# A two-layer diffusion transformer block on one core: the state-space mixer in three parts

## Chip, cores and metric

The kernel runs on one core of one Trainium2 chip. The metric is the device time of one execution in microseconds (us); lower is better. The kernel before has a median of 3212.48 us over 3 runs (3210.45 to 3216.32). TensorE is written PE (its weight loads PEld), VectorE DVE, ScalarE ACT, GpSimdE POOL, SyncE SP.

## What is computed

Two layers over 1024 tokens and 256 context tokens, 1024 channels. Layer 0 mixes by attention and retention, layer 1 by a state-space model (S5). Each layer ends with a squared-ReLU network. The change is in layer 1 and in what stands just before and after it:

```python
h_l = modulate(rmsnorm(x, norm1_g[l]), mod_l[:, 0], mod_l[:, 1])
h_c = modulate(rmsnorm(xc, norm1_g[l]), mod_c[0], mod_c[1])
...
def s5_mixer(h_c, h_l, p_f, p_b, d_skip, w_glu, need_ctx):
    ...
    y_cf, x_cf = s5_scan(u_c, ab_f, bb_f, c_f, x0)
    y_cb, x_cb = s5_scan(u_c[:, ::-1], ab_b, bb_b, c_b, x0)
    y_lf, _ = s5_scan(u_l, ab_f, bb_f, c_f, x_cf)
    y_lb, _ = s5_scan(u_l[:, ::-1], ab_b, bb_b, c_b, x_cb)
    out_l = s5_out(y_lf + y_lb[:, ::-1], u_l, d_skip, w_glu, h_l.dtype)
...
z = jax.nn.gelu(y).astype(dtype) @ w_glu
za, zb = jnp.split(z, 2, axis=-1)
return za * jax.nn.sigmoid(zb)
```

There are 64 groups of 16 channels with 64 complex states each. A state goes through the context and then through the tokens, once forward and once backward; the backward direction also begins with the context (reversed) and then takes the tokens from the last to the first. Context outputs of layer 1 are not needed.

## The kernel before

**Layout.** The residual x lies in SBUF as channels on partitions, 8 tiles (kt, oc) of 1280 columns: tokens 0 to 511 (block 0), tokens 512 to 1023 (block 1), context (block 2). Every large product is done in three passes of split operands (`mm3`, lines 70 to 72: high x high, low x high, high x low). Weights come by `split` (one transfer of 512 KB on SP at L1004, then the high part on ACT at L76 and the low part on DVE at L84), with three raw buffers.

**Networks.** `mlp` goes over 16 pairs of hidden tiles. `first` makes two hidden tiles (ReLU on ACT at L1053, squares, low part on POOL), `second` adds their share to the 8 output tiles; the sum goes from PSUM into x on DVE at L1070, unless the output is in `kept` and stays in its PSUM bank to the end. The network of layer 0 runs in two passes: blocks 0 and 2 (with six outputs of block 2 kept), then block 1 (three outputs kept).

**Side work.** While a network runs, a generator is stepped by `beat`: RA (0.07) steps per matrix product of 512 columns in the first pass, RB (0.125) in the second. The side work is, in order: modulation vectors of layer 1 (`ada_rest`, DVE), the S5 tables (`s5_gen`: powers, input and output matrices, lag matrices, cosines and sines, all written to DRAM tensors bst, cst, tst, csd), and the normalized inputs of blocks 0 and 2 (`s5_in`). What is left of it is drained after the second pass.

**The mixer's form.** Eight tokens make a chunk (128 token chunks, 32 context chunks). Within a chunk a 128x128 lag matrix Tt per group gives the direct part. Between chunks, states are turned by cosines and sines so that the recurrence becomes a real scan over chunks with decay R8. `s5_in` writes the inputs to the DRAM tensor ud, context twice, so that one row of 192 columns serves both directions (context, tokens, context).

**`s5_main`.** It runs alone on the core, 32 steps q of two groups. Per step: SP loads input matrices B, tables CS, output matrices C and two lag matrices Tt three steps ahead; ACT spreads CS (L1493, L1494); `states` does for each direction d four products of 160 columns (128x64 tiles, L1503), then on DVE a product with the tables (L1511), a sum (L1512) and two scans of 160 (L1516), and on DVE or POOL the turning back of 128 chunks (L1519); `outs`, two steps later, adds two lag products (L1531) and 32 products of 64x64 tiles (L1537: state half k times time half h, so all four quarters of the array). After four steps ACT takes two PSUM banks through GELU (L1542) into the tiles Y[kt, th]; th says which four of the eight places in a chunk.

**After it.** `glu` runs over th = 0, 1: 4 transposes per tile (L1573), split into yT (L76, L84), then 16 weight tiles of the gated product; sigmoid, gate, sum into x (L1592). Because of the order by place in the chunk, x is read with a stride of eight there and in the network of layer 1 (`xh`). Modulation rows 3, 4 and 5 of layer 1 are made beside `glu`.

**Order.** Instructions go to each engine in program order, and side work is put between the products where `beat` or `next(side)` stands. SP's queue is in order as well: a load that waits for a buffer holds back what is behind it.

## Time and profile before

| | |
|---|---|
| median of 3 runs | 3212.48 us |
| profiled execution, its own time | 3215.43 us |
| span of the profiled execution | 3213.6 us |
| mean granted clock of PE | 0.967 |
| DMA, mean of the span | 101 GB/s |

The page gives busy time of each engine over the span, and 40 slices of it. The timeline shows where the stages lie: layer 0's mixing up to about 1054 us, its network from there to 2080 us (second pass from about 1700), the normalization of block 1 to 2102, `s5_main` to 2285, `glu` to about 2500, the network of layer 1 to the end. In a row of groups the columns are line, engine, operation, output and inputs with their shapes, count, then busy time and mean of one in ns, then the engine's idle time before them and what ended it. In a row of waits: who waited, for whom, total, times, longest. A row of stages gives the busy time of each engine in the stretch, the granted clock, the DMA share and GB/s.

### The profile page before, as it was taken

What the parts mean: (1) busy time and instruction counts of PE and PEld (TensorE: products, weight loads), DVE (VectorE), ACT (ScalarE), POOL (GpSimd) and SP (SyncE); (2) the same over time, 40 slices, a digit from 0 to 9 for tenths busy, and PEclk for the clock granted to TensorE, in tenths of its full rate; (3) what the DMA queues carried; (4) which work ended last, traced back from release to release, by engine and by line L of the source; (5) the groups of instructions that cost most, each with busy time, mean ns of one, the idle gap of its engine ahead of it and who ended that gap; (6) DMA issues with size and microseconds to landing.
All of it is one profiled execution on the core that took longest, in us unless ns stands there. A gap on an engine that the chain in (4) does not pass through costs nothing. (4 is left out here: it accounts for less than half of the span.)

```text
span 3213.6 us, 45368 instructions
## 1 busy us (share of the span) xinstructions
PE 2968.0 (92%) x16683; PEld 2436.2 (76%) x16683; DVE 2111.0 (66%) x4014; ACT 1221.5 (38%) x2493; POOL 929.7 (29%) x902
## 2 busy tenths in 40 slices
PE   5899998899999998999997999967799999999998
PEld 3777777678878787887785778756678788888887
DVE  6777777687754688556468974378865555555555
ACT  6542222666762332222233664321334322222221
POOL 3642222455540113466326110123222111111111
PEclk8999999999999999999998999979999999999999
DMA  7132222301021452245426555287742111111111
GB/s 250 69 119 84 76 79 63 84 26 25 13 85 34 136 162 89 87 120 154 131 85 206 172 163 145 85 180 196 231 139 89 56 46 53 53 46 47 46 46 66
DMA packets 259039, 324.28 MB, mean 101 GB/s; under 512 B 72336, under 2 KB 179632, under 8 KB 258816
## 3 DMA queue, kind: packets, MB, share of 16 engines
q1 hardware_dynamic: 198352, 281.03, 29.0%
q10 hardware_dynamic: 59264, 36.84, 3.7%
q0 software_dynamic: 1200, 3.51, 0.4%
q8 instruction: 131, 2.15, 0.3%
q14 instruction: 92, 0.75, 0.1%
HBM read 267.96 MB, written 53.35 MB: 100 GB/s over the span
## 5 line engine op out<-in xcount | busy, mean ns | idle before, releaser
L84 POOL TENSOR_TENSOR al<-r,ah 128x512 fp32r<-128x512 f32 (+1 forms) x160 | 204.3, 1289 | 1191.5 <-ACT r L1057 1116.7
L1070 DVE SCALAR_TENSOR_TENSOR x<-b,mods,x 128x512 f32<-128x512 f32 (+1 forms) x483 | 457.5, 967 | 101.1 <-PE b L72 95.1
L84 DVE TENSOR_TENSOR ul<-mraw,uh 128x512 fp32r<-128x512 f32 x256 | 204.6, 803 | 429.3 <-ACT uh L76 428.7
L70 PE MATMUL b<-ah,dh 128*128 128x512 f32 (+1 forms) x1088 | 416.1, 383 | 21.4 <-ACT r L1053 10.2
L71 PE MATMUL b<-al,dh 128*128 128x512 f32 (+1 forms) x1088 | 413.7, 380 | 0.7 <-POOL al L84 0.7
L72 PE MATMUL b<-ah,dl 128*128 128x512 f32 (+1 forms) x1088 | 412.7, 380 | 0.5 <-DVE dl L84 0.4
L76 ACT ACTIVATE uh<-mraw 128x512 fp32r<-128x512 f32 x256 | 160.3, 628 | 453.3 <-PE b L71 261.3
L70 PE MATMUL b<-h2h,uh 128*128 128x512 f32 (+1 forms) x768 | 280.7, 366 | 21.8 <-DVE x L1070 11.6
L72 PE MATMUL b<-h2h,ul 128*128 128x512 f32 (+1 forms) x768 | 278.9, 364 | 18.6 <-DVE ul L84 18.4
L71 PE MATMUL b<-h2l,uh 128*128 128x512 f32 (+1 forms) x768 | 277.5, 361 | 0.0
L70 PEld LDWEIGHTS b<-ah,dh 128*128 128x128 f32 x1088 | 206.7, 190 | 64.8 <-DVE x L1070 11.6
L72 PEld LDWEIGHTS b<-ah,dl 128*128 128x128 f32 x1088 | 206.5, 190 | 40.5 <-DVE dl L84 1.9
L71 PEld LDWEIGHTS b<-al,dh 128*128 128x128 f32 x1088 | 207.0, 190 | 38.1 <-POOL al L84 1.1
L76 ACT ACTIVATE dh<-mraw 128x512 fp32r<-128x512 f32 x192 | 117.5, 627 | 248.2 <-PE b L71 119.6
L84 POOL TENSOR_TENSOR pl<-pe,ph 128x512 fp32r<-128x512 f32 (+1 forms) x128 | 158.3, 1246 | 154.9 <-ACT ph L76 86.8
L70 PE MATMUL b<-h3h,uh 128*128 128x512 f32 x512 | 202.0, 395 | 0.0
L71 PE MATMUL b<-h3l,uh 128*128 128x512 f32 x512 | 200.0, 391 | 2.0 <-DVE h3l L313 1.8
L72 PE MATMUL b<-h3h,ul 128*128 128x512 f32 x512 | 200.9, 393 | 0.0
L70 PEld LDWEIGHTS b<-h2h,uh 128*128 128x128 f32 x768 | 146.6, 191 | 50.5 <-DVE x L1070 14.2
L84 DVE TENSOR_TENSOR dl<-mraw,dh 128x512 fp32r<-128x512 f32 x192 | 150.5, 794 | 48.5 <-ACT dh L76 28.9
L72 PEld LDWEIGHTS b<-h2h,ul 128*128 128x128 f32 x768 | 146.4, 191 | 47.1 <-DVE ul L84 23.7
L1053 ACT ACTIVATE r<-b 128x512 f32<-128x512 f32 (+1 forms) x160 | 87.9, 550 | 244.9 <-PE b L72 170.8
(421 smaller groups left out, 7171.3 us busy)
## 6 DMA issues: line engine op xcount, KB each, us to landing
mraw<-in_w SPq DMA_DIRECT2D x192, 512.0 KB
aw<-in_adat SPq DMA_DIRECT2D x112, 256.0 KB
mraw<-in_glu SPq DMA_DIRECT2D x32, 512.0 KB
aw<-in_adat SPq DMA_DIRECT2D x96, 128.0 KB
CS<-csd SPq DMA_DIRECT2D x32, 320.0 KB
w<-in_adaw SPq DMA_DIRECT2D x32, 256.0 KB
wraw<-in_winr SPq DMA_DIRECT2D x32, 256.0 KB
cst<-oc ACTq DMA_DIRECT2D x64, 128.0 KB
```

The lines of the kernel that those rows point to most:

```text
L70: mm(o, s[0], m[0], start=start, stop=False)
L71: mm(o, s[0], m[1], start=False, stop=False)
L72: mm(o, s[1], m[0], start=False, stop=stop)
L76: self.nc.scalar.activation(o, x, AF.Copy)
L84: e.tensor_tensor(o, x, h.bitcast(F32), ALU.subtract)
L1053: nc.scalar.activation(r[:, :n], b[:, :n], AF.Relu)
L1070: nc.vector.scalar_tensor_tensor(o, as_x(b), self.M[:, l, 5, oc, s:s + 1], xs, op0=ALU.mult, op1=ALU.add)
```

## The change

The mixer is cut into three parts.

- `s5_first`, at the end of the side work beside the network's second pass: for each q the context in both directions (their end states go to the SBUF tensor `carry`) and the first 64 token chunks forward. Its sums go into Y[0, kt] without GELU. It starts when blocks 0 and 2 are normalized; a gate (`half`) keeps `s5_in` back until the network's first pass is written out.
- `s5_second`, alone: the last 64 chunks in both directions, from the carries; forward and backward share one PSUM bank, one scan of 260 columns, with a decay table that is zero at each start.
- `s5_third`, stepped by `next(side)` in `glu`'s first half: the first 64 chunks backward, added to Y[0, kt], and GELU at the end.

`s5_sums` multiplies state half k into output half k alone (64 chunks fit 64 rows). Y tiles now hold 512 consecutive tokens, so `glu` takes th = 1 first and x is read contiguously (`xh` is gone); the weights' rows are permuted on the host to match, and the transposes become 16 products of 64x64 tiles per tile, written with a stride. ud has 160 columns and another order, and `s5_in` writes each tile by eight transfers. RA becomes 0.09, RB 0.14; no output of block 1 is kept in PSUM; modulation rows 3 and 4 of layer 1 move to the side work of the first network. The loads of `s5_second` stand behind the last normalization and the rest of the side work.

```diff
-RA = 0.07
-RB = 0.125
+RA = 0.09
+RB = 0.14
...
 def s5_in(self, bi, x, tmp, b=None):
-            rows = self.ud[kt * P:(kt + 1) * P]
-            for c0 in ((32 + t0 // 8,) if t0 < NL else (0, 160)):
-                nc.sync.dma_start(rows[:, :, c0:c0 + nchunk], us.rearrange("p (s c) -> p s c", s=8))
+            for s in range(8):
+                nc.sync.dma_start(bass.AP(tensor=self.ud.tensor,
+                                          offset=self.ud.offset + 163840 * s + 1280 * kt + c0,
+                                          ap=[[160, 8], [10240, 16], [1, m]]), us[:, m * s:m * s + m])
...
+    def s5_spread(self, CS):
+        self.nc.scalar.activation(CS[:, 0], CS[:, 3], AF.Copy, scale=-1.0)
+        self.nc.scalar.activation(CS[:, 1], CS[:, 2], AF.Copy)
+
+    def s5_decay(self, o, mask, q, d):
+        self.nc.scalar.activation(o, mask, AF.Copy, scale=self.R8[:, 2 * q + d:2 * q + d + 1])
+
+    def s5_sums(self, o, q, k, y, C, start, stop):
+        mm = self.nc.tensor.matmul
+        R = slice(64 * k, 64 * k + 64)
+        for r, w in ((0, 0), (1, 0), (0, 1), (1, 1)):
+            mm(o[R, (q % 4) * P:(q % 4 + 1) * P], y[R, r, w], C[R, w], start=start and r + w == 0,
+               stop=stop and r + w == 2)
+
+    def s5_first(self):
...
+        def states(q):
...
+            for r in range(2):
+                for k in range(2):
+                    R = slice(64 * k, 64 * k + 64)
+                    mm(vb[R, P * r:P * r + 96], B[:, 0, r, R], u[:, k], start=True, stop=True)
+                    mm(vb[R, P * r + 96:P * r + P], B[:, 1, r, R], u[:, k, 31::-1], start=True, stop=True)
...
+        def outs(q):
...
+            for k in range(2):
+                mm(o[64 * k:64 * k + 64, (q % 4) * P:(q % 4 + 1) * P], u[:, k, 32:96], Tt[:, k], start=True, stop=False)
+                self.s5_sums(o, q, k, y, C, False, True)
...
+        for q in range(35):
+            if q < 32:
+                load(q)
+            yield
+            if 1 <= q < 33:
+                states(q - 1)
+            yield
+            yield
+            if q > 2:
+                outs(q - 3)
+            yield
...
+    def s5_second(self, p, last, rest):
...
+            CS = p.tile([P, 4, 2, 65], F32, tag="CS", name="CS", bufs=6)
...
+            v.tensor_tensor_scan(fl(z), fl(dec), fl(S), 0.0, ALU.mult, ALU.add)
...
+            for d in range(2):
+                for k in range(2):
+                    self.s5_sums(o, q, k, A[q, d], C[:, d], False, d == 1)
...
+        ut = p.tile([P, 64, 64], F32, name="ut")
         for _ in range(3):
             next(last)
-        inputs(0, 8)
         self.drain(last)
+        self.drain(rest)
+        for q in range(5):
+            load(q)
+            if q % 4 == 0:
+                inputs(2 * q, 8)
...
+    def s5_third(self, p):
...
+            CS = p.tile([P, 4, 65], F32, tag="CS", name="CS", bufs=3)
...
+            for k in range(2):
+                self.s5_sums(bank[0], q, k, A[q], C, True, True)
...
+        for q in range(35):
+            if q < 32:
+                load(q)
+            yield
+            if 1 <= q < 33:
+                states(q - 1)
+            yield
+            if q > 2:
+                outs(q - 3)
+            yield
+        for kt in range(KT):
+            nc.scalar.activation(self.Y[0, kt], self.Y[0, kt], self.gelu)
...
 def glu(self, p, x, after, sides):
-        for th in range(2):
+        for th in (1, 0):
...
-                for t in range(4):
-                    nc.tensor.transpose(tp[:, t * P:(t + 1) * P], self.Y[kt, th][:, t * P:(t + 1) * P], self.ident)
+                for t in range(8):
+                    for k in range(2):
+                        R, C = slice(64 * k, 64 * k + 64), slice(64 * t, 64 * t + 64)
+                        nc.tensor.matmul(tp[R, C], Y[R, C], self.ident[R, R], start=True, stop=True)
...
-                        if kt % 4 == 3:
-                            next(side, None)
+                        next(side, None)
...
+            self.drain(side)
...
 def run(self, stop=None):
-            yield from self.ada_rest(lambda: self.atile(name="aw"), rows, [(1, j) for j in range(3)])
+            yield from self.ada_rest(lambda: self.atile(name="aw"), rows, [(1, j) for j in range(5)])
             self.s5_setup(gp)
             yield from self.s5_gen(gp)
+            while not half:
+                yield
             for bi in (0, 2):
                 yield from self.s5_in(bi, x, tmp)
+            yield from self.s5_first()
...
-            self.mlp(0, mp, [(512, 512, 0)], hget2, x0, beat, after=st1.add,
-                     kept=[(512, oc) for oc in range(3)])
-        self.drain(side)
...
+            self.mlp(0, mp, [(512, 512, 0)], hget2, x0, beat, after=st1.add)
...
-            self.s5_main(p, self.s5_in(1, x, AT, st1.b))
+            self.s5_second(p, self.s5_in(1, x, AT, st1.b), side)
...
-            self.glu(mp, x, after, mods)
-            self.drain(mods)
+            self.glu(mp, x, after, {1: self.s5_third(sp), 0: mods()})
```

More of the change, by code (lines that the diff above doesn't have):

```diff
@@ L1477, in load @@
+    def s5_second(self, p, last, rest):
+        nc = self.nc
+        v, gp, mm = nc.vector, nc.gpsimd, nc.tensor.matmul
+        sl, A, bank = {}, {}, {}
         def load(q):
@@ L1479, in load @@
             nc.sync.dma_start(B, self.bst[:, q])
[L1480 to L1481 removed]
+            CS = p.tile([P, 4, 2, 65], F32, tag="CS", name="CS", bufs=6)
+            for d in range(2):
+                c0 = 31 if d else 95
+                nc.sync.dma_start(CS[:, 2:4, d], self.csd[:, 2 * q + d, :, c0:c0 + 65])
             nc.sync.dma_start(C, self.cst[:, q])
             Tt = self.atile(256, F32, "T").rearrange("p (k n) -> p k n", k=2)
[L1484 to L1487 removed]
+            self.s5_lag_rows(Tt, q)
@@ new lines, in states @@
+                self.s5_decay(dec[:, :, d], self.mask2[:, :, d], q, d)
+            S = p.tile([P, 2, 2, 65], F32, tag="ss", name="ss", bufs=2)
+            nc.scalar.activation(S[:, :, :, 0], self.carry[:, q].rearrange("p d w -> p w d"), AF.Copy)
+            vb = self.bank()
+            for r in range(2):
+                for k in range(2):
+                    R = slice(64 * k, 64 * k + 64)
+                    for d in range(2):
+                        u = ut[:, 2 * q + k] if d == 0 else ut[:, 2 * q + k, ::-1]
+                        mm(vb[R, P * r + 64 * d:P * r + 64 * d + 64], B[:, d, r, R], u, start=True, stop=True)
@@ new lines, in states @@
+            t = p.tile([P, 2, 2, 2, 64], F32, tag="st", name="st", bufs=2)
+            cs = CS.rearrange("p (r w) d c -> p r w d c", r=2)
+            for r in range(2):
+                v.tensor_tensor(t[:, r], vb[:, P * r:P * r + P].rearrange("p (d c) -> p d c", d=2).unsqueeze(
+                    1).to_broadcast([P, 2, 2, 64]), cs[:, 1 - r, :, :, 1:65], ALU.mult)
+            v.tensor_tensor(S[:, :, :, 1:65], t[:, 0], t[:, 1], ALU.add)
+            z = p.tile([P, 2, 2, 65], F32, tag="sz", name="sz", bufs=3)
@@ L1524, in outs @@
+            fl = lambda a: a.rearrange("p w d c -> p (w d c)")
+            v.tensor_tensor_scan(fl(z), fl(dec), fl(S), 0.0, ALU.mult, ALU.add)
+            nc.scalar.activation(self.carry[:, q, 1], z[:, :, 1, 64], AF.Copy)
+            for d in range(2):
+                A[q, d] = p.tile([P, 2, 2, 64], F32, tag=f"sy{d}", name="sy", bufs=3)
+                self.s5_turned(v if d else gp, A[q, d], z[:, :, d, 0:64], cs[:, :, :, d, 0:64], d)
         def outs(q):
-            B, C, Tt, CS = sl[q]
+            B, C, Tt, CS = sl.pop(q)
@@ L1527, in outs @@
             if q % 4 == 0:
-                ybank[0], ybank[1] = self.bank("z"), self.bank()
-            o = [ybank[k][:, (q % 4) * P:(q % 4 + 1) * P] for k in range(2)]
+                bank[0] = self.bank("z")
+            o = bank[0]
             for k in range(2):
-                mm(o[k], ut[:, 2 * q + k, 32:160], Tt[:, k], start=True, stop=False)
+                mm(o[64 * k:64 * k + 64, (q % 4) * P:(q % 4 + 1) * P], ut[:, 2 * q + k], Tt[:, k], start=True,
+                   stop=False)
@@ L1545, in s5_main, with inputs @@
-        for q in range(3):
-            load(q)
-        ut = p.tile([P, 64, 192], F32, name="ut")
+                for k in range(2):
+                    self.s5_sums(o, q, k, A[q, d], C[:, d], False, d == 1)
+            if q % 4 == 3:
+                y = self.Y[1, q // 4] = self.atile(name="y")
+                nc.scalar.activation(self.s5_places(y), self.s5_pairs(o), self.gelu)
+        def inputs(g0, n):
+            nc.sync.dma_start(ut[:, g0:g0 + n], self.ud[:, g0:g0 + n, 96:160])
+        ut = p.tile([P, 64, 64], F32, name="ut")
@@ L1548, in s5_main @@
         for _ in range(3):
             next(last)
-        inputs(0, 8)
         self.drain(last)
+        self.drain(rest)
+        for q in range(5):
+            load(q)
+            if q % 4 == 0:
+                inputs(2 * q, 8)
         for q in range(32):
-            spread(q)
             states(q)
-            if q % 4 == 0 and q < 28:
-                inputs(2 * q + 8, 8)
-            if q < 29:
-                load(q + 3)
+            if q % 4 == 0 and 2 * q + 16 < 64:
+                inputs(2 * q + 16, 8)
+            if q < 27:
+                load(q + 5)
@@ L1566, in glu @@
+    def glu(self, p, x, after, sides):
         nc, I = self.nc, self.I
-        for th in range(2):
+        for th in (1, 0):
             yT = {}
@@ L1754, in after @@
                 sums[th].add(oc)
-                if th == 0 and oc == KT - 1:
-                    g0.append(nrm2(0))
-                if th and oc:
+                if th and oc == KT - 1:
+                    g0.append(nrm2(1))
+                if not th and oc:
                     next(g0[0], None)
```

219 lines of the change are left out of this document (137 added, 82 removed).

## The prediction

> **What bounds the kernel now.** I read the page's first part, then the busy time of each engine by stage, because the change moves work between stages.
>
> ```profile
> PE 2968.0 (92%) x16683; PEld 2436.2 (76%) x16683; DVE 2111.0 (66%) x4014; ACT 1221.5 (38%) x2493; POOL 929.7 (29%) x902
> ```
>
> ```profile
> core 0: us, PE busy (x) PEld busy (x) DVE busy (x) ACT busy (x) POOL busy (x), PEclk, DMA share, GB/s
> 1054.00:1700.00 646.00, 603.38 (x3717) 513.51 (x3715) 417.53 (x770) 194.16 (x398) 244.59 (x247) 0.97 0.40 124
> 1700.00:2081.00 381.00, 358.14 (x1522) 288.36 (x1522) 259.63 (x486) 189.54 (x323) 83.87 (x60) 0.96 0.52 155
> 2081.00:2103.00 22.00, 5.85 (x28) 5.45 (x30) 5.96 (x10) 10.79 (x16) 1.20 (x1) 0.54 0.58 88
> 2103.00:2285.00 182.00, 140.65 (x2693) 116.26 (x2690) 154.15 (x289) 37.76 (x95) 59.88 (x46) 0.92 0.78 196
> 2285.00:2300.00 15.00, 3.77 (x28) 3.54 (x27) 12.38 (x52) 3.03 (x8) 0.00 (x0) 0.69 0.82 277
> 2300.00:2520.00 220.00, 210.98 (x930) 169.09 (x929) 138.55 (x271) 94.79 (x144) 50.98 (x30) 0.98 0.39 123
> 2520.00:3214.00 694.00, 683.19 (x2995) 561.76 (x2993) 381.88 (x376) 179.68 (x306) 86.83 (x63) 1.00 0.16 50
> ```
>
> The rows are the first network's two passes (to 1700, to 2081), the step to the mixer, the mixer, the step to the gated product, the gated product, the second network. PE bounds the networks and the gated product (94 to 98%). In the mixer PE has 41 of 182 us free and DVE leads. The two steps waste 27 us more. The waits of the mixer and DVE's groups there say the same:
>
> ```profile
> POOL sy L1519 <- DVE sz L1516: 97.7, 25, 26.5
> PE z L1537 <- POOL sy L1519: 33.0, 24, 3.1
> PE b L1503 <- DMA ut<-ud: 14.3, 1, 14.3
> ```
>
> ```profile
> L1516 DVE TENSOR_TENSOR_SCAN sz<-R,st 128x160 f32<-128x160 f32 x128 | 60.8, 523 | 0.5
> L1511 DVE TENSOR_TENSOR st<-b,CS 128x640 f32<-128x640 f32 x64 | 50.0, 808 | 36.6 <-issue 18.6 <-ACT CS L1494 9.2 <-PE b L1503 8.8
> L1512 DVE TENSOR_TENSOR st<-st 128x320 f32<-128x320 f32 x64 | 31.8, 525 | 0.0
> L1519 DVE TENSOR_TENSOR sy<-sz,CS 128x512 f32<-128x512 f32 x22 | 19.4, 881 | 0.1
> ```
>
> PE waits for the turned states, these for the scan: a DVE chain. So the change takes work from a DVE-bound stretch and puts it where PE is full. Its worth is what the mixer loses, less what PE gains elsewhere, and PE's price decides.
>
> **PE's price for the tiles.** Here is PE in the mixer, in order of time (start, length):
>
> ```profile
> 2200.02 0.27 PE L1537 MATMUL z<-C,sy 64*64 64x128 f32 x1
> 2200.22 1.31 PE L1503 MATMUL b<-ut,B 128*64 128x160 f32 x16
> 2201.46 0.49 PE L1531 MATMUL b<-T,ut 128*128 128x128 f32 x2
> ...
> 2202.20 0.27 PE L1537 MATMUL z<-C,sy 64*64 64x128 f32 x1
> 2202.21 0.27 PE L1537 MATMUL b<-C,sy 64*64 64x128 f32 x1
> 2202.22 0.27 PE L1537 MATMUL z<-C,sy 64*64 64x128 f32 x1
> 2202.22 0.27 PE L1537 MATMUL b<-C,sy 64*64 64x128 f32 x1
> 2202.32 0.27 PE L1537 MATMUL z<-C,sy 64*64 64x128 f32 x1
> ```
>
> ```profile
> L1537 PE MATMUL z<-C,sy 64*64 64x128 f32 x1024 | 74.7, 291 | 40.3 <-POOL sy L1519 33.0 <-DVE sy L1519 6.8
> ```
>
> Four 64x64 tiles start within 0.02 us, and the next four 0.11 us later. Each matrix product is two records, two passes (the loops write 512 into z, the row has 1024), so a round of four products takes two periods, 0.22 us, and L1537 costs 8 rounds = 1.75 us per pair q. Before, all four quarters of the array work. After, `s5_sums` multiplies half k of the states into half k of the output: two diagonal quarters, and the four products of one half follow each other on the same tile before the other half comes. The number of products per q stays 32 over the three parts (8, 16, 8), but a round holds two at most.
>
> A change of tile shape costs too. Here a visit of small tiles in the network (L1433, 32 records, 8 periods = 0.87 us):
>
> ```profile
> 1320.97 0.28 PE L72 MATMUL b<-h2h,ul 128*128 128x256 f32 x1
> 1321.18 1.08 PE L1433 MATMUL b<-oc,bb 64*32 64x128 f32 x32
> 1322.18 0.50 PE L70 MATMUL b<-h2h,uh 128*128 128x512 f32 x1
> ```
>
> From 1321.18 to 1322.18 are 1.00 us, 0.13 over the work, and the start was late by 0.09. I take 0.125 us for each change of shape (bounds 0.09 to 0.18).
>
> *First part* (beside the first network's second pass), per q. States: 96 and 32 columns for each half and component; at 0.85 ns per column and pass (0.11 over 128) two components are 4 x 128 x 0.85 = 0.44. Then lag(0), sums(0), lag(1), sums(1): two lags of 0.22 and two chains of 4 x 0.22, with a change of shape between each, so that nothing of one half runs beside the other: 2.18. Six or seven changes, the states' two among them, are 0.87. Sum 3.5 us, **+112 us** for 32 q. Nothing covers it: PE is the bound there. Bounds: 1.55 us (50 us) if the halves overlap and changes cost nothing; 4 us (128 us).
>
> *Third part* (beside the gated product's first half), per q: states 4 x 64 x 0.85 = 0.22, sums in four rounds with the halves side by side 0.87, four changes 0.5: 1.6 us, **+51 us**. Bounds 35 (no changes) and 72 (the halves one after the other, 0.65 more per q).
>
> *Second part* (alone), per q. PE: states 0.44, lags 0.22, sums 8 rounds 1.75, two changes 0.25: 2.65. DVE: L1511 and L1512 give about 1 ns per column and 0.15 fixed; two products of 256 columns (0.41 each), a sum of 260 (0.42), one scan of 260 (0.66, at L1516's 2 ns per column), one turn of 256 (0.42): 2.3 us, against 154 / 32 = 4.8 before. DMA: 196 GB/s at a share of 0.78 is 251 GB/s when all are busy; B and C 262 KB each, the two tables 133, lags 131 and inputs 66 KB are 854 KB, 3.4 us. So DMA takes DVE's place as the bound, at about 3.6 us: 115, and 6 for filling and draining as before, 121 instead of 182: **-61 us**. Bounds -85 (DVE, 2.3) and -42 (PE one half after the other, 4.0 us).
>
> **The writes and the steps.** `s5_in` now writes each tile by eight transfers instead of one or two: 192 for 32. SP issues them in order with the weights' loads:
>
> ```profile
> L1461 SPq DMA_DIRECT2D ud<-us x8: 513/595/3197, 2090.2 to 2103.3; - x8
> ```
>
> ```profile
> L1472 SPq DMA_DIRECT2D ut<-ud x64: 302/429/1687, 2093.4 to 2249.9; - x64
> ```
>
> ```profile
> L1485 SPq DMA_DIRECT2D T<-tst x64: 574/580/1180, 1946.0 to 2270.3; - x64
> ```
>
> The new form (128 pieces of 256 or 128 bytes) is not in the trace. L1472 moves 128 pieces in 0.30 to 0.43 us, L1485 in 0.58. With 0.05 between two, I take 0.475 us (0.35 to 0.63), nearest to L1472.
>
> ```profile
> 2080.02 0.39 PE L71 MATMUL b<-al,dh 128*128 128x512 f32 x1
> 2080.25 0.39 PE L72 MATMUL b<-ah,dl 128*128 128x512 f32 x1
> ...
> 2102.50 0.54 PE L1503 MATMUL b<-ut,B 128*64 128x160 f32 x2 [14.32 <-DMA ut<-ud]
> ```
>
> *Step to the mixer.* Before, 22 us pass between the network's last product and the first state. The first write is issued at 2090.2. After, 64 writes take 30 us, and behind them stand load(0) (six issues) and the input (together 3 us; they were issued ahead before) and a landing of 2 to 3 us: 2126 instead of 2102.5, **+23 us** (+15 to +36). What is left of the first part fills some of PE's time there.
>
> *Same writes in the second pass* (blocks 0 and 2): 128 x 0.475 = 61 us of SP, asked for in 18 steps of the side work. A step comes every 1 / 0.14 products of 0.23 us = 1.6 us, so within 29 us. Weights are fetched two or three tiles ahead, some 12 us; behind the writes they come late. The lower end is nothing, the upper 61 - 29 - 12 = 20 (44 at 0.63). **+15 us**.
>
> *Buffers.* In the first part loads take nearly all buffers of the two activation sizes, in the third the table has three; SP waits for a turned state of three q earlier, and the next weight load stands behind it. Nothing shows this wait. 0 to 70 us (2.4 us in each of 16 gated weight tiles, 1 us per q in the first part); **+10**.
>
> *Transposes and layout of the gated product.*
>
> ```profile
> L1573 PE MATMUL b<-ident,y x64: 270/273/474, 2284.4 to 2399.6; 128*128 128x128 f32 x64
> ```
>
> ```profile
> L76 ACT ACTIVATE yh<-b 128x512 fp32r<-128x512 f32 x16 | 8.4, 608 | 0.0
> L1457 ACT ACTIVATE us<-u,mods 128x512 f32<-128x512 f32 x8 | 8.1, 1134 | 1.7 <-DVE u L264 1.7
> ```
>
> Four transposes of one record at 0.11 become sixteen small products, eight pairs of two passes of 64 columns (0.055): 0.88 for 0.44, 16 times, +7. yh and yl are now written with a stride of eight, as L1457 writes: 1.13 for 0.61, eight in a row ahead of each half, +4 each. **+15 us** (5 to 20).
>
> Costed at nothing: SP's 7 loads per q of the first part (covered by some 10 us per q), DVE's and ACT's extra work in the networks (DVE 260 of 381 us busy, and PE gets longer), two modulation rows moved into the first pass, 45 more residual sums since no bank is kept, and the second network, whose sums become contiguous: PE is 683 of 694 there, so 1 us at most. If DVE's cover fails, the 23 us that PE idles in the second pass could double. The side work has 57 + 211 + 18 + 140 = 426 steps; the passes give 2253 x 0.09 + 1536 x 0.14 = 418. So it ends with the network but for the last sums, and the gate on the second pass never waits (268 steps lie ahead of it, 203 are done when it opens).
>
> **Sum.** 3215.4 (the profiled execution, span 3213.6) + 112 + 51 - 61 + 23 + 15 + 10 + 15 = 3380. That execution is 3 us over the median of 3212.5, so about **3377 us**. Without PE's 163 us the rest is zero to within 2 us: steps and writes eat the mixer's gain.
>
> **Rivals.**
> *Strict order on PE:* if a product that waits for its tile holds back the other half behind it, only the seams of the chains overlap: 7 rounds in place of 4 for a chain pair. Third part +21, second 4.0 us per q, +13: 3411. For it: no row shows four products in a row on one tile. Against it: z and b alternate within 0.02 us though each product has two passes, so second passes waited and let others by. [...]
> *SP as the bound:* 0.63 per write and the full buffer waits: +13 in the step, +29 in the pass, +28 of the 70: 3447. For it: SP is in order and everything new is issued there; against: it is idle most of a network's time.
> *Faster:* the first part fills PE's idle time in the first network. Price: halves overlap and changes are free, so 50 us of PE go into the 66 us (43 + 23) that PE waits there for DVE and ACT; third 35, mixer -67 (DMA at 3.4), step +15, transposes +7: 3202, -0.3%. It decides only if first and third part lengthen PE by less than about 40 us together. Against it: the waits come in bursts, and a change of shape visibly costs.
> *It does not do what it says:* the side work runs late and is drained alone ahead of the second part; for each 10 steps missing 8 us more. Within the forecast.
>
> **How the numbers follow.** Forecast 0.57, strict order 0.14, SP 0.17, faster 0.08, no change 0.04 (the faster case with the step at +23). The range 3270 to 3450 leaves out the last two and some of SP's end; its lower end is the first part at its lower bound (-62), nothing for buffers and writes (-25) and DVE's bound in the mixer (-24). A measurement of this kernel tells about 0.2% from no change. Slower 0.88, same 0.04, faster 0.08.
>
> **What would show it.** The second pass of the first network longer by some 130 us, with about 3.5 us of small tiles per q between its products; the mixer's loop near 120 us with the DMA share at 0.9; a step of over 40 us with SP issuing ud writes; the gated product's first half 50 us longer. Wrong would be: small tiles of both halves starting together in the first part, writes at 0.3 us or less, or a second pass that does not grow.

## The result, and the profile after

After the change the kernel takes 3495.7 us (median of 4 runs, 3487.8 to 3497.0) against 3211.6 before (4 runs on the same chip): a ratio of 1.088, interval 1.086 to 1.090. The forecast was 3377 us, range 3270 to 3450. The direction was right; the loss is 284 us where 165 were forecast, and the time lies above the range.

The page's first part now reads as follows (engine, busy time, share, instructions). PE has 212 us more than the 2968.0 before, DVE 60 us less than its 2111.0: the trade that the change makes.

```profile
PE 3179.9 (91%) x18027; PEld 2586.0 (74%) x18027; DVE 2050.5 (59%) x4082; ACT 1324.2 (38%) x2916; POOL 939.1 (27%) x956
```

The busy time by stage, same columns as in the prediction. The stages are the first network's two passes, the step to the mixer, the second part, the step to the gated product, its two halves, and the last network.

```profile
1054.00:1725.00 671.00, 603.51 (x3674) 509.20 (x3673) 457.71 (x835) 194.21 (x398) 267.92 (x260) 0.95 0.42 139
1725.00:2292.00 567.00, 487.66 (x2649) 376.39 (x2647) 332.94 (x625) 234.98 (x495) 86.75 (x77) 0.92 0.43 129
2292.00:2354.00 62.00, 18.38 (x84) 14.05 (x83) 7.40 (x11) 11.75 (x24) 1.41 (x2) 0.53 0.28 66
2354.00:2507.00 153.00, 130.45 (x1625) 114.62 (x1626) 74.27 (x160) 44.30 (x193) 24.61 (x32) 0.86 0.68 186
2507.00:2518.00 11.00, 11.00 (x299) 10.59 (x297) 5.46 (x7) 7.38 (x13) 0.00 (x0) 1.00 0.19 64
2518.00:2688.00 170.00, 170.00 (x1410) 127.57 (x1410) 100.45 (x218) 88.87 (x204) 46.38 (x50) 1.00 0.49 144
2688.00:2778.00 90.00, 90.00 (x407) 74.32 (x406) 42.77 (x59) 37.17 (x60) 19.47 (x13) 1.00 0.25 88
2778.00:3493.00 715.00, 706.61 (x3098) 580.20 (x3097) 287.69 (x400) 193.64 (x329) 90.22 (x65) 1.00 0.15 51
```

The stages that take the work have grown, all three with PE full before: the first pass (671 for 646), the second (567 for 391), the gated product's first half (170 for 101). The mixer's own loop has shrunk, but to 153 and not to 121. The three longest kinds of waits of PE behind the first pass, in us in total, times and longest:

```profile
PE b L1543 <- DMA u<-ud: 44.7, 1, 44.7
PE b L1615 <- DMA ut<-ud: 43.3, 1, 43.3
PE z L1636 <- ACT y L1643: 18.7, 6, 4.3
```

The first did not exist before, the second was 14.3 us (L1503), the third is new too. The first has its cause on SP, here in order of time:

```profile
1880.53 79.52 SPq L1464 DMA_DIRECT2D ud<-us  x128
1960.15 0.40 SPq L1521 DMA_DIRECT2D B<-bst  x1
```

All 128 writes of blocks 0 and 2 stand in one row, 0.62 us each, with no load between them. From 1918 to 1963 PE has nothing to do.

One q of the first part on PE, in order of time (start, length):

```profile
2101.16 0.40 PE L72 MATMUL b<-h2h,ul 128*128 128x512 f32 x1
2101.49 0.39 PE L1543 MATMUL b<-u,B 128*64 128x96 f32 x4
...
2102.20 0.49 PE L70 MATMUL b<-h2h,uh 128*128 128x512 f32 x1
2102.53 0.40 PE L71 MATMUL b<-h2l,uh 128*128 128x512 f32 x1
...
2104.87 0.40 PE L72 MATMUL b<-h2h,ul 128*128 128x512 f32 x1
2105.20 0.43 PE L1565 MATMUL z<-T,u 128*64 128x128 f32 x2
2105.56 1.08 PE L1508 MATMUL z<-C,sy 64*64 64x128 f32 x8
2106.57 0.43 PE L1565 MATMUL z<-T,u 128*64 128x128 f32 x2
2106.93 1.08 PE L1508 MATMUL z<-C,sy 64*64 64x128 f32 x8
2107.95 0.49 PE L70 MATMUL b<-h2h,uh 128*128 128x512 f32 x1
2108.28 0.40 PE L71 MATMUL b<-h2l,uh 128*128 128x512 f32 x1
```

Two chains of eight records follow each other, 1.08 us each. Each visit of small tiles also costs more than its work. L1543 starts 0.33 us after the last product, where the next product would start after 0.23, and the first product behind a visit (L70) takes 0.33 to the next start as well. From the product ahead of a visit to the second one behind it, less the 0.47 of two products, the states cost 0.90 us and the outputs 2.94. Of these 3.84 us per q, 0.44 and 2.18 are work by the prediction's count, so 1.22 are left for seven changes of tile shape, 0.17 each (an estimate from these rows). The steady stretches of this pass agree: a pair of hidden tiles (96 products, at 0.14 steps each and four steps per q 3.36 q) takes 35.0 us in place of 22.1, which is 3.84 us per q again.

Where the 279 us between the two profiled spans lie (from the starts of products in both traces; time over its products is a stretch's length less its products, 0.2335 us for each of 512 columns):

| stretch | before | after | change |
|---|---|---|---|
| ahead of the first network | 1075.1 | 1072.3 | -2.8 |
| first network up to the end of the tables: time over its products | 105.0 | 146.6 | +41.6 |
| first network behind that: time over its products | 4.0 | 176.4 | +172.4 |
| last product to first state (leftover of the first part 19.0, then no work 43.3) | 21.9 | 62.3 | +40.4 |
| mixer, second part: first state to last sum | 182.0 | 156.2 | -25.8 |
| step to the gated product | 16.2 | 7.4 | -8.8 |
| gated product, first half | 100.9 | 169.8 | +68.9 |
| gated product, second half | 90.9 | 90.9 | 0 |
| last network and end | 721.0 | 714.5 | -6.5 |

### The profile page after: what moved, and what is told of

It is laid out like the page before. It is cut to its first block, busy times and chain, and to the rows that moved or that the text cites. A ratio compares the mean times of both kernels' runs of the same rounds, so it can differ in the third digit from the quotient of the medians.

```text
span 3492.9 us, 49581 instructions
## 1 busy us (share of the span) xinstructions
PE 3179.9 (91%) x18027; PEld 2586.0 (74%) x18027; DVE 2050.5 (59%) x4082; ACT 1324.2 (38%) x2916; POOL 939.1 (27%) x956
## 4 chain that ended last, share of the span: by engine, by line
PE 47%; DVE 9%; DMA 5%; SPq 3%; issue 3%; POOL 2%; ACT 1%; ACTq 0%; DVEq 0%; POOLq 0%
PE b L70 13%; PE b L72 12%; PE b L71 12%; PE z L1508 5%; SPq L1464 2%; DVE aw L216 1%; DMA ww<-pbd 1%; DVE x L1070 1%; DMA aw<-in_adat 1%; DVE dl L84 1%; DVE ul L84 1%; DVE ta L1324 1%; PE z L1565 1%; DVE ta L1327 1%; POOL oc L1403 1%
## 5 line engine op out<-in xcount | busy, mean ns | idle before, releaser
L1070 DVE SCALAR_TENSOR_TENSOR x<-b,mods,x 128x512 f32<-128x512 f32 (+1 forms) x530 | 383.5, 729 | 238.4 <-PE b L72 237.9
L70 PE MATMUL b<-ah,dh 128*128 128x512 f32 (+1 forms) x1152 | 448.2, 389 | 22.6 <-ACT r L1053 12.5
L72 PE MATMUL b<-ah,dl 128*128 128x512 f32 (+1 forms) x1152 | 440.7, 384 | 3.2 <-DVE dl L84 3.2
L71 PE MATMUL b<-al,dh 128*128 128x512 f32 (+1 forms) x1152 | 441.0, 383 | 0.7 <-POOL al L84 0.7
L70 PE MATMUL b<-h2h,uh 128*128 128x512 f32 (+1 forms) x768 | 285.9, 372 | 27.9 <-ACT uh L76 27.9
L70 PEld LDWEIGHTS b<-ah,dh 128*128 128x128 f32 x1152 | 220.4, 191 | 75.9 <-ACT r L1053 15.3
L72 PEld LDWEIGHTS b<-ah,dl 128*128 128x128 f32 x1152 | 220.2, 191 | 47.2 <-DVE dl L84 4.8
L71 PEld LDWEIGHTS b<-al,dh 128*128 128x128 f32 x1152 | 220.3, 191 | 40.1 <-POOL al L84 1.1
L1508 PE MATMUL z<-C,sy 64*64 64x128 f32 x2048 | 221.6, 291 | 3.7 <-POOL sy L1497 3.7
L1508 PEld LDWEIGHTS z<-C,sy 64*64 64x64 f32 x2048 | 185.9, 142 | 34.8 <-issue 27.1
L1497 POOL TENSOR_TENSOR sy<-sz,CS 128x256 f32<-128x256 f32 x96 | 73.4, 764 | 503.2 <-DVE sz L1624 86.5
L70 PE MATMUL b<-h3h,uh 128*128 128x512 f32 x512 | 202.3, 396 | 0.0
```

The source lines that it names most:

```text
L70: mm(o, s[0], m[0], start=start, stop=False)
L71: mm(o, s[0], m[1], start=False, stop=False)
L72: mm(o, s[1], m[0], start=False, stop=stop)
L1070: nc.vector.scalar_tensor_tensor(o, as_x(b), self.M[:, l, 5, oc, s:s + 1], xs, op0=ALU.mult, op1=ALU.add)
L1497: e.tensor_tensor(y if not back else y[:, :, :, ::-1], z.unsqueeze(2).to_broadcast([P, 2, 2, 64]), cs[:, :, ::-1], ALU.mult)
L1508: mm(o[R, (q % 4) * P:(q % 4 + 1) * P], y[R, r, w], C[R, w], start=start and r + w == 0, stop=stop and r + w == 2)
```

## The experiments

Theory at the start: A, PE pays for chains whose halves do not run side by side; C, SP's burst of writes holds the loads back; E, the higher rate of side work lengthens the first pass; G, the two banks z make PE wait for the GELU. Line numbers shift by a few from kernel to kernel.

### Halves in turn (e1_alternate) and by two (e1b_by_two)

```diff
-        for r, w in ((0, 0), (1, 0), (0, 1), (1, 1)):
-            mm(o[R, ...], y[R, r, w], C[R, w], ...)
+        for r, w in ((0, 0), (1, 0), (0, 1), (1, 1)):
+            for k in range(2):
+                R = slice(64 * k, 64 * k + 64)
+                mm(o[R, ...], y[R, r, w], C[R, w], ...)
```

> The change's kernel, but the products of the two halves of each output tile alternate in program order (in the first part both lags first). Theory A (a half's four dependent products hold the other half back; four quarters of the array are not shared): in the first part 20 periods of 0.109 us per q become 10 and two changes of tile shape go, 1.3 us per q or 43 us less between 1724 and 2310; in the third part 12 periods become 8, 0.44 us per q or 14 us less of the gated product's first half (169.7); in the second part 16 to 24 us less of 153. Together about 3420 us against 3496. Rival B (the price is in the changes of tile shape and in the bursts of the other engines, not in the order of the halves): first part less than 15 us shorter, third less than 5, all about 3475.

> As e1_alternate, but two products of one half, then two of the other. Theory A1 (PE looks ahead past a waiting product by about two products): same as e1_alternate within 5 us. Theory A2 (strict order: nothing passes a product that waits for its tile): 10 periods per pair of chains in place of 8, so 0.22 us per q more than e1_alternate in the third part (7 us) and as much again in the first (7) and twice that in the second (14, if PE is the bound there), some 20 to 28 us over e1_alternate.

Measured: 3418.1 us (1.062 of before, 1.060 to 1.064) and 3416.9 (1.062, 1.059 to 1.064). The first network's second pass is 38.1 us shorter (567.3 to 529.2), the leftover behind it 8.6 (19.0 to 10.4), the gated product's first half 15.6 (169.8 to 154.2); by two it is 156.1. The third part's sums in order of time, after the change and then with the halves in turn:

```profile
2602.07 0.39 PE L72 MATMUL b<-yh,ul 128*128 128x512 f32 x1
2602.39 1.58 PE L1508 MATMUL z<-C,sy 64*64 64x128 f32 x16
2603.90 0.50 PE L70 MATMUL b<-yh,uh 128*128 128x512 f32 x1
```

```profile
2557.83 0.39 PE L72 MATMUL b<-yh,ul 128*128 128x512 f32 x1
2558.15 1.09 PE L1509 MATMUL z<-C,sy 64*64 64x128 f32 x16
2559.17 0.50 PE L70 MATMUL b<-yh,uh 128*128 128x512 f32 x1
```

The same sixteen records take 1.02 us in place of 1.51, from their start to the next product's. And the first part's outputs of one q with the halves in turn, 1.39 us from L1566 to the next product where 2.75 stood above:

```profile
2102.42 0.40 PE L72 MATMUL b<-h2h,ul 128*128 128x512 f32 x1
2102.74 0.44 PE L1566 MATMUL z<-T,u 128*64 128x128 f32 x4
2103.11 1.09 PE L1509 MATMUL z<-C,sy 64*64 64x128 f32 x16
2104.13 0.50 PE L70 MATMUL b<-h2h,uh 128*128 128x512 f32 x1
```

Theory A holds, in each of its terms: 43 us were expected in the first part (47 came, pass and leftover together), 14 in the third (15.6), 16 to 24 in the second (22.6: first state to last sum takes 133.6 for 156.2). Order by two costs 1.9 us in the third part where a strict order would cost 7, and nothing in the total. With the change's order the second chain does not wait for the end of the first: after the change its first record starts at 2602.885, just behind the first chain's fifth record (2602.880), which is its third product. So two products of each chain run alone and two beside the other chain: 12 periods of 0.109 us, where halves side by side take 8. Whether PE lets the products by or the builder of the program had put them in that order, no view shows.

### Writes on POOL's queue (e2_writes_pool), and one transfer per tile (e5_layout)

```diff
+                e = nc.sync if bi == 1 and s % 2 else nc.gpsimd
-                nc.sync.dma_start(bass.AP(tensor=self.ud.tensor, ...
+                e.dma_start(bass.AP(tensor=self.ud.tensor, ...
```

```diff
-            for s in range(8):
-                nc.sync.dma_start(bass.AP(tensor=self.ud.tensor, offset=..., ap=[[160, 8], [10240, 16], [1, m]]),
-                                  us[:, m * s:m * s + m])
+            nc.sync.dma_start(self.ud[kt * P:(kt + 1) * P, :, c0:c0 + m], us.rearrange("p (s c) -> p s c", s=8))
...
-            nc.sync.dma_start(u, self.ud[:, 2 * q:2 * q + 2, 0:96])
+            for k in range(2):
+                self.s5_u(u[:, k], 2 * q + k, 0, 96)
```

> The change's kernel, but the ud writes of blocks 0 and 2 (128) are issued by POOL, those of block 1 (64) by SP and POOL in turn. Theory C (SP, in order at 0.62 us for each such write, holds the weights back): the 45-us stall of PE in the second pass of the first network (1918 to 1963) goes or falls below 10 us, and the step to the mixer (43.7 us without a main product) is 15 to 20 us shorter, as 32 writes of 0.62 go to another queue: about 3435 us. Rival D (the transfers themselves, not their issue, take the time: 128 pieces of 256 bytes per write on the engines that move the weights as well): stall and step stay within 10 us, about 3490.

> The change's kernel with the state inputs stored by channel as in the kernel before, so that a tile is written by one transfer in place of eight (24 writes for 192) and read by one transfer per group of channels (192 reads for 72). Theory C (the time goes into SP's issue of the burst of writes, 0.62 us each): the 45-us stall of the second pass falls below 8 us, the step's 43 us without a product become 20 to 28, total 3425 to 3440, although 120 reads of some 0.43 us are added in places where SP has time. Rival I (issue time is only moved: reads delay the first and second part as much): total within 20 us of 3496.

Measured: 3456.3 us (1.074, 1.072 to 1.077) with the writes on POOL, 3406.3 (1.061, 1.058 to 1.063) with one transfer per tile. On POOL the step's gap fell from 43.3 to 23.9 us as expected, but only 23 us of the second pass came back, so the total stays above the 3435 us of theory C. PE's waits there and POOL in order of time show why:

```profile
PE z L1509 <- POOL sy L1498: 14.0, 2, 13.4
PE b L1544 <- DMA u<-ud: 12.3, 1, 12.3
```

```profile
1926.32 37.51 POOL L1465 DMA_DIRECT2D ud<-us  x64
1963.84 0.74 POOL L1498 TENSOR_TENSOR sy<-sz,CS 128x256 f32<-128x256 f32 x1
```

A write costs POOL 0.59 us, as much as SP, and now the first part's turned states stand behind the burst. With one transfer per tile the second pass is 54.8 us shorter (512.5), and of PE's waits only this is left at the step:

```profile
PE b L1617 <- DMA ut<-ud: 11.6, 1, 11.6
```

So theory C is right and rival D falls: the time is the issue of 128 instructions, not the bytes. The reads that were added (192 for 72) cost nothing that shows here, though they do in e8_all (below); rival I falls too. The gain, 89 us against 56 to 71 expected, is larger because the second pass regains 54.8 us, more than the stall of 45, and the step falls to 11.6 us where 20 to 28 were expected: a write of 1024 pieces costs SP hardly more than one of 128 (last section).

### Rates of the side work (e3_rates, b1_rates)

```diff
-RA = 0.09
-RB = 0.14
+RA = 0.07
+RB = 0.175
```

> The change's kernel with 0.07 and 0.175 steps of side work per product in place of 0.09 and 0.14: the total of steps stays. Theory E (the first pass is longer by 34.5 us because 45 more steps of side work lie in it, whose DVE and ACT work comes ahead of what PE waits for): first pass back to 636 to 645 us from 669.5, second pass about as much longer as those steps cost there, 10 to 35 us, total 3470 to 3500. Rival F (it is longer because of the new modulation rows' form, the masks or the place of the buffers, not the rate): first pass stays within 8 us of 669.5.

Measured: 3456.7 us (1.074, 1.071 to 1.076). First pass 600.9, second 598.4, against 652.3 and 567.3. Most of that only moves work, so the passes are compared up to the end of the table generation instead. The three rows are that stretch before, after, and with the lower rate:

```profile
1075.00:1876.00 801.00, 743.72 (x4285) 624.28 (x4286) 574.12 (x1097) 283.04 (x556) 296.98 (x279) 0.96 0.44 137
```

```profile
1072.00:1876.00 804.00, 717.19 (x4126) 598.93 (x4126) 592.43 (x1153) 274.63 (x538) 294.59 (x276) 0.95 0.44 143
```

```profile
1076.00:1887.00 811.00, 745.20 (x4276) 624.95 (x4277) 614.51 (x1181) 286.75 (x559) 303.89 (x279) 0.95 0.45 146
```

The tables take some 800 to 811 us at both rates, but at 0.09 PE gets through 159 fewer records in them than before (x4126 for x4285). At the higher rate the network waits for the side work's DVE and ACT instructions instead of hiding them (PE waits for these two engines for 62.5 us in that stretch before, 86.2 after, 70.8 with 0.07); time over the products up to that point is 105.0 us before, 146.6 after, 118.8 with 0.07. So theory E holds, though the total lies below the 3470 to 3500 us that it gave, and 28 of the 42 us come back; the other 14 go with the two modulation rows that the change moved there or with the higher second rate (not tried apart). The leftover of the first part is 11 us shorter as well (19.0 to 8.0), and so is the second part with its last step (11.5).

The same idea on the kernel before, whose side work ends 140 us ahead of the second pass's end:

```diff
-RA = 0.07
-RB = 0.125
+RA = 0.05
+RB = 0.12
```

> The kernel before, with 0.05 and 0.12 steps of side work per product in place of 0.07 and 0.125 (its side work ends at 1942 of 2081 us, so there is room for 45 steps later). Theory E (a step of side work taken out of the first pass gives about 1 us there, as e3_rates showed: 51 us for 45 steps, and costs 0.7 in the second): first pass 20 to 45 us shorter than 615, second pass 10 to 30 longer than 391, total 3190 to 3205. Rival P (the first pass of the kernel before has no such cost, for its steps there are others): both passes within 8 us, total 3208 to 3216.

Measured: 3224.5 us (1.0036, 1.0023 to 1.0049), slower by a third of a per cent. First pass -25.7, second +27.9; time over the products up to the end of the tables is 107.1, as before (105.0). In the profiled execution 10.8 us of the loss lie ahead of the first network (1085.9 us for 1075.1), where the edit changes nothing; the two passes together lose 2. Theory E went too far here: between 0.07 and 0.05 steps per product, a step taken out of one pass costs as much in the other.

### The second part's banks (e4_second_b)

```diff
             if q % 4 == 0:
-                bank[0] = self.bank("z")
+                bank[0] = self.bank()
```

> The change's kernel, but the output banks of the second part come from the pool of the banks b, not from the two banks z. Theory G (PE waits six times, 18.7 us in all, for the GELU that empties the bank before the last): these waits go, the second part is 15 to 19 us shorter than 153, total about 3478. Rival H (the GELU is late because ACT is, so the wait moves to the products that take the next b bank): less than 5 us.

Measured: 3452.6 us (1.075, 1.072 to 1.077), 43 us less, more than twice what was expected. The waits are gone, and first state to last sum is 118.6 us for 156.2. The granted clock explains the rest. Here is PE in the second part after the change behind one of the six waits for the GELU (five of them took 2.89 us, the first 4.28), with the stretch at once behind it and the next one, then the kernel with the other banks:

```profile
2412.39 0.69 PE L1636 MATMUL z<-T,ut 128*64 128x128 f32 x2 [2.89 <-ACT y L1643]
```

```profile
2412.40:2418.50 6.10, 6.10 (x51) 5.77 (x52) 2.31 (x5) 2.31 (x11) 0.93 (x2) 0.50 0.81 228
2418.60:2430.00 11.40, 11.40 (x159) 9.62 (x157) 4.61 (x10) 2.59 (x12) 1.55 (x2) 1.00 0.80 221
```

```profile
2347.00:2384.00 37.00, 35.41 (x489) 31.11 (x491) 22.78 (x50) 11.03 (x52) 6.79 (x9) 0.87 0.88 238
2384.00:2460.00 76.00, 75.95 (x1111) 65.85 (x1108) 49.88 (x108) 32.64 (x137) 17.03 (x22) 1.00 0.82 225
```

Behind the wait of 2.89 us that ends at 2412.39 PE's granted clock is 0.50 for 6.1 us (51 records), then 1.00 (159 records in 11.4 us). Behind the other four of 2.89 us it is 0.50 or 0.51 over the same 6.1 us and 1.00 after them; behind the one of 4.28 us it is 0.62 over 5.9 us. The part's mean clock is 0.86 over 153 us after the change and about 0.96 over 113 us here, 21 us of clock lost against 5. With the 18.7 us of waits that makes 35 of the 37.6 us. What lowers the clock and what brings it back, no view shows.

### The third part alone (e7_third_alone)

```diff
             side = sides[th]
+            if th:
+                self.drain(side)
```

> The change's kernel, but the third part runs to its end between the transposes and the first products of the gated product's first half, not beside these. Theory J (beside hides nothing, for PE is full in both): PE's products of that half go back to 101 us and the third part takes 65 to 85 us alone, total within 12 us of 3496. Rival K (the part alone would be bound by DVE, POOL or its loads, so that running it beside hides much): the part alone takes 100 us or more, total 3525 or more.

Measured: 3529.8 us (1.099, 1.096 to 1.102), 34 us more. The first half's products go back to 104.5 us; alone the part takes some 101 us, the gap between second part and products growing by that much. By number this is rival K, which gave 100 us or more and a total of 3525 or more; theory J's 65 to 85 us and its total are missed. The stages say otherwise of the cause (the part alone, then the first half's products):

```profile
2517.40:2617.00 99.60, 85.51 (x737) 74.36 (x736) 44.63 (x106) 31.22 (x130) 23.35 (x35) 0.63 0.46 120
2617.00:2714.00 97.00, 97.00 (x423) 78.65 (x422) 46.61 (x106) 32.84 (x55) 20.14 (x14) 0.94 0.37 126
```

PE is busy for most of the part, DVE, ACT and POOL for less than half, but at a clock of 0.63: 37 us of clock lost in 99.6, about the difference between 101 alone and 65 beside (169.8 less 104.5). So the rows speak for theory J's mechanism: beside the products the part hides next to nothing, it only keeps the clock up (1.00 beside, 0.63 alone). This reading is worked out from the rows and not shown; no run holds the clock up with the part alone.

### The edits together (e8_all, e9_reads_pool, e10_pairs)

e8_all joins halves in turn, one transfer per tile, the rates of e3_rates and the banks of e4_second_b. e9_reads_pool has POOL issue the second part's reads. e10_pairs takes two q at a time in the first and third part:

```diff
-                self.s5_u(ut[:, g], g, 96, 64)
+                self.s5_u(ut[:, g], g, 96, 64, gp)
```

```diff
-        for q in range(35):
-            if q < 32:
-                load(q)
-            yield
+        for q in range(0, 36, 2):
+            for i in (q, q + 1):
+                if i < 32:
+                    load(i)
+                yield
...
+                states(q - 2)
                 states(q - 1)
...
+                outs(q - 4)
                 outs(q - 3)
```

> The four edits together: halves in turn, a tile written by one transfer, 0.07 and 0.175 steps per product, second part on the banks b. If the gains add: 3496 - 83 (halves) - 62 (writes) - 40 (rates) - 17 (banks) = 3294; the rates' gain overlaps the writes' (both shorten the wait behind the first network), so 3290 to 3325. All theories so far say that it stays above the kernel before (3212), since the products of the first and third part, 2.3 and 1.9 us per q, are still paid in stretches where PE is full, against some 80 us gained in the second part and the steps.

> The kernel of e8_all, but the 64 reads of the second part's inputs are issued by POOL in place of SP. Theory L (in e8_all SP is the bound of the second part: eight reads of 0.6 us stand in a row ahead of the loads of B, and PE waits 26.6 us for B): the waits for B fall below 8 us, the second part's 127 us from first to last state become 105 to 115, DMA's 854 KB per q being next, total 3285 to 3297. Rival M (the transfers themselves are late): 122 us or more, total above 3300.

> The kernel of e9_reads_pool, but first and third part take two q at a time: two sets of states in a row, then two sets of outputs in a row, so three changes of tile shape of ten go for each two q of the first part, and four of eight in the third. Theory N (a change costs about 0.1 us of PE each): 5 us less in the second pass, 6 us less in the gated product's first half, total 8 to 14 us less than e9_reads_pool. Rival O (changes cost nothing to speak of, or the longer hold of the buffers costs as much): within 5 us of e9_reads_pool or longer.

Measured: 3306.8 us (1.029, 1.027 to 1.031), 3280.0 (1.021, 1.019 to 1.022) and 3268.2 (1.017, 1.016 to 1.019). The edits add up within their overlap. In e8_all PE waits 26.6 us in the second part for B, behind rows of eight reads on SP; with the reads on POOL 4.6 us of that are left in the part, and it takes 110.1 us in place of 133.5 from first state to last sum (the total is 5 us below theory L's range). Pairs take 10.9 us from the gated product's first half and 10.0 from the second pass, about twice what was expected. With 64 changes of tile shape gone in the one and 48 in the other, a change costs 0.17 to 0.21 us, as the rows of the first part gave; the second part gives 5 back. In e10_pairs PE no longer fills the second part, and DMA is busy for 0.88 of it:

```profile
2194.00:2300.00 106.00, 92.75 (x1526) 79.00 (x1528) 75.00 (x155) 41.97 (x183) 47.51 (x73) 0.92 0.88 230
```

It still ends 55 us above the kernel before. Against that kernel the mixer and the step behind it are 76 us shorter there, while the first part still costs some 73 us in the second pass and the third 43 in the gated product; the tables cost 14 more and the step 6. The repairs make the change cheaper, not a gain.

### All turns on POOL in the kernel before (b2_rates_turns)

```diff
-                e = gp if (2 * q + d) % 3 else v
+                e = gp
```

> The kernel of b1_rates with all 64 turns of the mixer on POOL (1.3 us each) in place of two of three, so that DVE, which leads there with 154 of 182 us, loses 19.4 us. Theory Q (DVE is the bound of the mixer before): mixer 182 to 165-172 us, total 10 to 17 us below b1_rates. Rival R (a turn takes 0.5 us longer on POOL, and PE waits for turns as it is, 33 us): mixer 180 us or more, total not below b1_rates.

Measured: 3216.2 us (1.0002, 0.9992 to 1.0013), 8 us less than b1_rates, but not in the mixer: that takes 181.6 us for 181.9, first state to last sum. In the two profiled executions the difference lies ahead of the first network (1077.0 us for 1085.9), where the edit changes nothing. DVE's groups there (busy, mean ns of one), in b1_rates and with all turns on POOL:

```profile
L1511 DVE TENSOR_TENSOR st<-b,CS 128x640 f32<-128x640 f32 x64 | 50.0, 809 | 36.4 <-issue 22.7 <-PE b L1503 8.9 <-DMA T<-tst 4.9
L1512 DVE TENSOR_TENSOR st<-st 128x320 f32<-128x320 f32 x64 | 31.8, 524 | 0.0
```

```profile
L1511 DVE TENSOR_TENSOR st<-b,CS 128x640 f32<-128x640 f32 x64 | 49.6, 808 | 44.7 <-issue 14.8 <-PE b L1503 13.8 <-ACT CS L1494 11.0
L1512 DVE TENSOR_TENSOR st<-st 128x320 f32<-128x320 f32 x64 | 45.4, 745 | 0.0
```

The turns' 19.4 us leave DVE, but L1512 takes 13.6 us more, 745 ns for 524, so DVE's busy time falls by 8 only. L1511, which reads one operand from a bank, keeps its time. And PE waits for turns as before (33.9 us for 34.7). Rival R holds in the mixer, though its total (not below b1_rates) did not come. That the mixer before is held by the way from a state through scan and turn to the product, more than by the sum of DVE's work, is the reading that is left, but a turn on POOL is also longer than one on DVE (1.4 us for 0.9), and DMA, at a share of 0.78 to 0.80 there, was not tried. No kernel of this study is faster than the one before.

## Why the prediction was right in direction and wrong in size

By the two profiled spans the change costs 279 us where 165 were forecast. Three terms of the sum carry most of the 114 us between them: the first pass, put at nothing (42), the writes in the second pass (38 too little) and the second part's gain (35 too much).

**First part, +112.** Measured 3.84 us per q against 3.5, 123 us. With the writes' 53 us (next) this makes 176 of the 172.4 us that the first network loses behind the tables. The model of one half behind the other was right, and e1_alternate shows it. The changes of shape were sized too small, 0.125 us each where the rows give 0.17: the prediction counted the late start of a visit and its end, but not the product behind it, which is late too.

**Writes in the second pass, +15.** They cost 53 us, by e5_layout. Two steps of it failed. The price was taken at 0.475, nearest to the read of L1472; it is 0.62, the upper bound, which the prediction itself had priced at 44 us. And the cover was overrated: 29 us of steps and 12 of prefetch were taken off, but the writes came as one row without a load between them. The rival "SP as the bound" had the right mechanism.

**First pass, costed at nothing.** It cost 42 us, the largest error. The prediction called DVE's and ACT's work covered and looked only at whether the steps fit in number. It did not ask what a higher rate does to the products beside it; the three windows of the rates show it, for 28 of the 42 us. The cause of the other 14 stays open. The prediction's "If DVE's cover fails" was about the second pass.

**Step, +23.** From the last product to the first state it is +40.4 us, of which 19.0 are the first part's leftover; the +21.4 that remain are near the forecast by luck. The mechanism is there, on SP:

```profile
2308.92 39.90 SPq L1464 DMA_DIRECT2D ud<-us  x64
```

But the 64 writes take 39.9 us where 30 were forecast, the same price that was too low, and the first comes 17.4 us behind the last product (2291.5) where it came 9.9 before, with the leftover on PE in between.

**Second part, -61.** Measured -25.8. Two steps failed. The prediction did not look at the two banks z, emptied by a GELU that stands behind the carry's copy on ACT: with other banks the part takes 118.6. And it had the two halves run side by side, PE at 2.65 us per q: with the halves in turn, and the banks as they were, the part takes 133.6. That 118.6 comes near the 121 of the forecast is luck, for the bound there was PE and not, as the prediction had it, DMA: PE is busy 75.95 of 76 us in that kernel, at a DMA share of 0.82, and needs 3.7 us per q (118.6 / 32).

**Third part, +51, and transposes, +15.** The first half grew by 68.9. The chains take 12 periods of 0.109 us where the prediction put the two halves side by side (8) and its rival a strict order (14); that is 14 us, and the changes of shape the rest. The transposes did grow, from 3.65 us (32 records) to 7.7 (256 records) ahead of the second half, but the step has the other sign, 8.8 us shorter. Before, the transposes waited in it for DVE, which had sums of the modulation rows to do ahead of yl (L216, 11 us from 2284.5 to 2298.7):

```profile
PE b L1573 <- DVE yl L84: 11.2, 1, 11.2
```

After the change no L216 stands there and the wait is gone. The move of two modulation rows, costed at nothing, gained that; no run moves them alone.

**Buffers, +10.** Nothing that shows: PE is busy 170 of 170 us beside the third part, and from 1994 to 2312 us, where most of the first part runs, it waits 0.5 us in all.

**Strict order on PE, as a rival.** The chains do interfere, as it said, but only over a few products: e1b_by_two is no slower than e1_alternate (3416.9 us for 3418.1). In which order PE gets the products, no view shows.

**What bounds the mixer.** "A DVE chain" was right as a chain and wrong as a load: b2_rates_turns takes 8 us of busy time from DVE and the mixer stays (181.6 us).

The section on the kernel says that instructions go to each engine in program order. The traces show it only roughly: the third part's first copies on ACT (L1690, at 2358.39 and 2360.91 us) run inside the second part, ahead of its last GELU (L1643, at 2510.44).

## What to carry to other kernels

Here work moved from a stretch that waits into one where PE is full cost its whole PE time there (3.84 us per q in the first part). The products that use half the array cost twice as much: in periods of 0.109 us, an estimate from the rows, the sums of one q come to 1.75 us before and to 0.87, 1.75 and 0.87 in three parts at best. Price that first, and only then what the emptied stretch gains. Count the instructions of a queue, not its bytes, wherever a burst is put in front of loads (128 writes held SP for 79.5 us, and PE waited 44.7 us for a load behind them). Behind a wait of 2.89 us PE ran at a clock of 0.50 for 6.1 us, so a stall of 3 us in a loop can be worth removing even where the engine looks 85% busy (130 of 153 us in the second part).

## What was not expected of the hardware

The price of a write on its queue did not go by its pieces: SP issues one of 128 pieces in 0.57 us (0.62 from start to start) and one of 1024 pieces (e5_layout, 24 writes) in 0.51 to 0.94, half of them in less than 0.53; POOL takes 0.59 for 128 pieces. The row of L1461 in the prediction (1024 pieces, 513 ns at least) had shown it.

PE ran at a mean granted clock of 0.63 for 99.6 us of e7_third_alone although it was busy 86% of the time and waited at most 2.2 us at a stretch; from 2600 to 2617 us the clock was 0.50 with PE busy for 15.23 of the 17 us. In the second part after the change a clock of 0.50 came behind waits of 2.89 us; here it came without a wait as long as that. What sets it, no view shows.

DVE was held up beside POOL: L1512, with both operands in SBUF, went from 524 to 745 ns when POOL's share of the mixer rose from 42 to 64 turns. The mean mixes two cases: in b2_rates_turns 26 of the 64 lie mostly beside a turn on POOL and take 1.13 us on average, and the 37 that touch none take 0.48; in b1_rates these are 5 and 42 of 64. L1511, which reads one operand from a bank, stayed at 809 and 808 ns. What holds L1512 up, no view shows. The scans (L1516), which read decay and sums from SBUF, met it less often with all turns on POOL: 10 of 128 take more than 0.8 us in b1_rates and 4 in b2_rates_turns, where L1512 has 3 and 21 of 64.

Two chains of dependent products on two tiles, one written behind the other, ran beside each other from the first one's third product on (2602.885 us after the change): with four in a row, sixteen records took 1.51 us, with two in a row or one in turn 1.02 to 1.07. The order in which PE gets them is read from the kernel; no view shows it.
